# A tuned hybrid decoder layer on one core: the seventh and eighth input-projection weights of the first tile are loaded into a buffer of their own

## The chip, the core and the metric

The kernel runs on one core of a Trainium2 chip. The metric is device time in microseconds (us), from one execution of the whole program; the figure to beat is the median of three executions. The profile comes from one further execution.

Five engines work side by side, each through its own instruction list, strictly in the order of that list: TensorE (PE, with its weight loads PEld), VectorE (DVE), ScalarE (ACT), GpSimd (POOL) and SyncE (SP), which here does nothing but issue DMA transfers. An instruction that waits for a semaphore holds up all that stand behind it on its engine.

## The reference, cut to what matters

One decoder layer over 2048 tokens of 1024 channels, all in float32:

```python
hn   = rms_norm(x, mix_pre_g)
proj = hn @ w_in                              # q, k, v and the GLU input u
attn = sliding_window_attention(q, k, v, attn_sinks, rel_bias)
a, gate = split(u); c = a * sigmoid(gate)     # 512 channels
c = silu(layer_norm(causal_depthwise_conv31(c)))  @ w_conv_pw
h  = x + rms_norm(concat(attn, c) @ w_out, mix_post_g)
hn = rms_norm(h, ffn_pre_g)
h  = h + rms_norm((silu(hn @ w_gate) * (hn @ w_up)) @ w_down, ffn_post_g)
```

The change touches only the loading of a part of `w_in` for the first 512 tokens.

## The kernel before, in words

**Tiles.** The 2048 tokens are cut into four tiles of T = 512. Stage A of tile t (`stage_a`, names with `@A`) projects the tile with 14 units of `w_in`; a unit is 128 output channels, its weight a 128x1024 float32 block of 512 KB. Units 0 to 7 are the four GLU pairs (gate and value), 8 is k, 9 is v, 10 to 13 are q. Stage B (`@B`) is the attention of a tile, stage C (`@C`) its convolution, whose 31 taps run on DVE one by one into tiles called `fc`, stage W (`@W`) the output projection, stages H, F, G the feed-forward part. Stage J multiplies `w_conv_pw` with its half of `w_out` beforehand.

**Three products for one.** float32 accuracy is made from three passes of float32r: every operand is held as a high part and a low part. `split_w` (line 130) makes them from a raw weight: ACT copies the raw block to the high part (line 133), DVE subtracts that from the raw block to get the low part (line 136; it shows as line 85, the helper that records DVE operations), and SP stores the low part to HBM (`lo_in`, line 137), from where tiles 1 to 3 load it (line 132) instead of making it again. `three` (line 174) then issues, per 128 input channels, weight high by data high, weight high by data low, weight low by data high. So of each unit's 24 matmuls the first two need the high half alone and the third needs DVE's subtraction.

**The first tile.** Units 0 to 3 come as `w_four`, in quarters beside the first input blocks (`four`, line 343). From unit 4 on, `proj` (line 337) calls `kweight` (line 146), that calls `weight` (line 140), which takes a tile `raw` from a pool of two, has SP load the unit into it (line 143), and splits its two halves into two tiles `w` of a pool of six. As `raw` has two buffers, the load of unit 6 can't start before unit 4 has been split, nor that of unit 7 before unit 5 has been. The norm of the tile is applied after the first matmuls: `post` yields the row factors, and the GLU of the first pairs (`glu`, line 374; tiles `fa`) starts when they are there.

**What sets the order.** The order of each engine's list is not written by hand. The Tile framework schedules the recorded operations with priorities and a timeline of its own; lanes of side work (taps, attention, tails, joins) are pumped between the projections by estimated costs (`yield` values). A new or moved operation early on can so change the lists for a good while behind it. Taps have low priority and are put where DVE seems free.

**The tile `yt`.** It is a pool of one buffer, 128 x 2048 float32. Its users are stage J (line 702), the tails of the convolution (line 627) and the feed-forward part. In the trace stage J is the first that writes it, at 197.94 us.

Of the kernel before, what the change touches and what calls it, by code (L numbers as in the profile page):

```python
# [25 lines left out]
P = 128  # L26
T = 512
# [10 lines left out]
def layer_kernel(ctx, tc, x, xT, cols, rows, sinks, relb, onehot, w_in, w_four, w_pw, w_out, w_gate, w_up, w_down, out):  # L38
    nc = tc.nc
# [9 lines left out]
    def nm(s):  # L49
        uid[0] += 1  # L50
        return f"{s}@{lab[0]}_{uid[0]}"
# [3 lines left out]
    def t_(tag, shape, dt=F32):  # L55
        return sb.tile(list(shape), dt, tag=tag, name=nm(tag), bufs=BUFS[tag])
# [83 lines left out]
    def weight(src, low, made, raw=None, on_pool=True):  # L140
        if raw is None:
            raw = t_("raw", (P, 2, T))
            nc.sync.dma_start(raw, src)
        return [split_w(raw[:, n], "w", low[n], made, on_pool) for n in range(2)]

    def kweight(u, made, raw=None):
        hs = weight(w_in[u].rearrange("p (a b) -> p a b", a=2), lo_in[u], made, raw, False)
        return [(hs[k // 4][:, 0, (k % 4) * P : (k % 4 + 1) * P], hs[k // 4][:, 1, (k % 4) * P : (k % 4 + 1) * P]) for k in range(KC)]
# [41 lines left out]
    def three(o, pairs, first=True, last=True):  # L190
        n = 3 * len(pairs)
        i = 0
        for (sh, sl), (mh, ml) in pairs:
            for a, b in ((sh, mh), (sh, ml), (sl, mh)):
                mat(o, a, b, start=first and i == 0, stop=last and i == n - 1)
                i += 1
# [119 lines left out]
    def split_x(t, xs, rb, ks):  # L316
# [12 lines left out]
            hn.append(hk)  # L329
        return hn  # L330

    def stage_a(t, hn, done_with, hooks, post=None):
        L = f"A{t}"
        lab[0] = L
        rb = None

        def proj(u, bank_of=mm):
            w = kweight(u, t > 0)
            o = bank_of()
            for k in range(KC):  # L340
                three(o, [(w[k], (hn[k][:, 0], hn[k][:, 1]))], k == 0, k == KC - 1)
            return o
# [47 lines left out]
        for c in range(4):  # L390
            if post and c == 0:
                os = yield from four()
            if post and c < 2:
                continue
            og = proj(2 * c, tr if post and c == 2 else mm)
            if post and c == 2:
                rb = next(post)
                for j in range(2):
                    next(glu(j, *os[2 * j : 2 * j + 2]))
            half = glu(c, og, None)  # L400
            next(half)
            yield 5.2
            step(2 * c)
            half.send(proj(2 * c + 1, tr if post and c == 2 else mm))
            yield 5.2
            step(2 * c + 1)
        done_with("S")
        lab[0] = L
        ok = proj(8)
        if t:  # L410
            act(kz[:, :, 0:P], kz[:, :, T : T + P].bitcast(F32), AF.Copy)
# [1086 lines left out]
    for t in range(NT):  # L1498
        hooks = {}
        if t + 1 < NT:  # L1500
# [27 lines left out]
            if t < 2:  # L1528
                hooks.update({(9 if t == 0 else 8) + i: lambda i=i, f=pair_of: f(i) for i in range(4)})
        run(mark(stage_a(t, hn_a[t], (lambda n: lb.until(f"{n}{t-1}")) if t else (lambda n: None), hooks,  # L1530
                         None if t else norm_x(0, x0, sum_squares(0, x0))), f"A{t}"))
        for n, part in zip((f"S{t}", f"B{t}"), stage_b(t)):
# [97 lines left out]
```

## Time and profile before

| what | us |
|---|---|
| median of three executions | 1910.04 |
| lowest, highest | 1907.92, 1913.49 |
| the profiled execution, device time | 1913.71 |
| its span, first to last instruction | 1912.0 |
| outside of the span | 1.71 |
| PE busy in the span | 1889.1 (99%) |
| DVE busy | 1498.7 (78%) |
| ACT busy | 968.6 (51%) |
| POOL busy | 200.7 (10%) |
| mean share of the 16 DMA engines, 439.36 MB | 230 GB/s |
| mean granted PE clock | 0.999 of full speed |

In a row of the timeline stand the start and the length in us, the engine, the line, the operation, what it writes and reads by the program's names (number of the buffer left out), shapes and the count of merged instructions; in brackets how long the engine stood idle before it and who released it. A merged row's length reaches to the end of its last instruction, and PE's matmuls overlap: 128x512 matmuls follow each other at some 0.23 us although one takes 0.39 us. In the table of stages there stand the busy us and the counts of each engine, then the granted clock, the DMA share and the rate. In the list of waits stand the sum, the count and the longest.

### The profile page before, as it was taken

Reading aid. Unit: us, or ns where it says so; the run is one execution under the profiler, and the core shown is the slowest. Engines: PE = TensorE matmul, PEld = TensorE weight load, DVE = VectorE, ACT = ScalarE, POOL = GpSimd, SP = SyncE. Lnnn points to the kernel's source line nnn. Section 1 sums busy time; section 2 is a strip of 40 time slices with the busy share of each in tenths; the row PEclk is TensorE's granted clock in tenths of the full one; section 3 lists DMA queues with packets and bytes.
Section 4 is the critical chain, followed back from the end, with each engine's and each line's share of the span. In section 5 each row is a group of like instructions: output and inputs, shape, how many; then the busy total and the mean of one; then the engine's idle time right before and its main releaser. Section 6 shows DMA issues by size and latency. Waiting matters only on the chain.

```text
span 1912.0 us, 26682 instructions
## 1 busy us (share of the span) xinstructions
PE 1889.1 (99%) x8714; PEld 1530.7 (80%) x8714; DVE 1498.7 (78%) x2806; ACT 968.6 (51%) x1912; POOL 200.7 (10%) x247
## 2 busy tenths in 40 slices
PE   9999999999999999999999999999999999999998
PEld 7777777777778888887888888888888888888886
DVE  6999999998876999988999866787566665455558
ACT  5365445667567433433446583676443343345452
POOL 2010001210000000000000100010033233211002
PEclk9999999999999999999999999999999999999999
DMA  9886756769678776786696696798554543376663
GB/s 334 305 279 231 243 178 188 232 228 344 208 243 288 245 259 237 255 272 222 193 314 205 202 342 204 252 329 313 179 176 151 163 138 127 116 255 188 206 218 130
DMA packets 227644, 439.36 MB, mean 230 GB/s; under 512 B 22664, under 2 KB 48688, under 8 KB 227504
## 3 DMA queue, kind: packets, MB, share of 16 engines
q1 hardware_dynamic: 206192, 403.04, 63.5%
q10 hardware_dynamic: 19392, 28.32, 4.1%
q0 software_dynamic: 1920, 6.29, 0.9%
q8 instruction: 68, 1.11, 0.2%
q14 instruction: 72, 0.59, 0.1%
HBM read 318.54 MB, written 119.02 MB: 229 GB/s over the span
## 4 chain that ended last, share of the span: by engine, by line
PE 72%; DVE 14%; DMA 8%; issue 3%; ACT 1%; POOL 1%; SPq 1%; DVEq 0%; ACTq 0%; POOLq 0%
PE mm@F L108 38%; PE mm@G L108 19%; PE mm@A L108 6%; DVE fc@C L85 5%; PE tr@W L108 4%; PE mm@W L108 2%; PE tr@B L108 1%; DMA glu@C<-glu_scr 1%; DVE sm@G L85 1%; DMA chl@F<-w_gate 1%; DVE w@F L85 1%; DMA p@X<-w_four 1%; DVE tr@B L493 1%; DVE p@B L496 1%; DMA p@A<-x 1%
## 5 line engine op out<-in xcount | busy, mean ns | idle before, releaser
L85 DVE SCALAR_TENSOR_TENSOR fc@C<-glu@C,colt,fc@C 128x512 f32<-128x512 f32 x480 | 353.0, 752 | 1.6
L108 PE MATMUL mm@F<-hl@H,w@F 128*128 128x512 f32 x1056 | 254.4, 390 | 0.0
L108 PEld LDWEIGHTS mm@F<-hl@H,w@F 128*128 128x128 f32 x1056 | 197.9, 188 | 41.9 <-ACT fa@F L1049 0.8
L108 PE MATMUL mm@G<-hl@G,hl@G 128*128 128x512 f32 x924 | 227.6, 393 | 0.1
L891 ACT ACTIVATE w@F<-chl@F 128x512 fp32r<-128x512 f32 x220 | 135.6, 625 | 134.5 <-PE mm@F L108 128.9
L108 PE MATMUL mm@G<-w@G,hl@G 128*128 128x512 f32 x876 | 199.8, 389 | 0.6 <-DVE w@G L85 0.6
L108 PEld LDWEIGHTS mm@G<-hl@G,hl@G 128*128 128x128 f32 x924 | 171.3, 188 | 36.2 <-ACT hl@G L891 0.5
L108 PE MATMUL mm@A<-hl@A,w@A 128*128 128x512 f32 x792 | 193.3, 394 | 1.9 <-DVE w@A L85 1.7
L108 PEld LDWEIGHTS mm@G<-w@G,hl@G 128*128 128x128 f32 x876 | 164.3, 188 | 35.3 <-DVE w@G L85 1.0
L108 PEld LDWEIGHTS mm@A<-hl@A,w@A 128*128 128x128 f32 x792 | 146.6, 188 | 35.3 <-DVE w@A L85 2.2
L85 DVE TENSOR_TENSOR w@F<-chl@F,w@F 128x512 fp32r<-128x512 f32 x198 | 145.6, 739 | 32.7 <-ACT w@F L891 32.2
L108 PE MATMUL mm@F<-ql@H,w@F 128*128 128x512 f32 x528 | 130.4, 391 | 1.8 <-ACT w@F L891 1.4
L108 PE MATMUL mm@F<-mid@H,w@F 128*128 128x512 f32 x528 | 130.2, 390 | 0.0
L108 PE MATMUL mm@F<-p@H,w@F 128*128 128x512 f32 x528 | 129.2, 389 | 0.0
L108 PE MATMUL mm@F<-x@H,w@F 128*128 128x512 f32 x528 | 128.0, 391 | 0.0
L108 PEld LDWEIGHTS mm@F<-ql@H,w@F 128*128 128x128 f32 x528 | 98.4, 188 | 24.0 <-ACT w@F L891 2.3
L108 PEld LDWEIGHTS mm@F<-p@H,w@F 128*128 128x128 f32 x528 | 99.0, 188 | 20.8 <-ACT at@F L1149 0.4
L108 PEld LDWEIGHTS mm@F<-x@H,w@F 128*128 128x128 f32 x528 | 98.6, 188 | 21.1 <-issue 0.8
L108 PEld LDWEIGHTS mm@F<-mid@H,w@F 128*128 128x128 f32 x528 | 99.0, 188 | 20.5
L85 DVE TENSOR_TENSOR w@G<-raw@G,w@G 128x512 fp32r<-128x512 f32 x72 | 50.7, 705 | 67.5 <-ACT w@G L891 66.8
L108 PE MATMUL mm@W<-w@W,hl@W 128*128 128x512 f32 x384 | 97.9, 398 | 2.8 <-DVE hl@W L85 2.1
L133 ACT ACTIVATE w@A<-raw@A 128x512 fp32r<-128x512 f32 x104 | 63.0, 625 | 67.4 <-DMA raw@A<-w_in 38.4
(319 smaller groups left out, 3190.7 us busy)
## 6 DMA issues: line engine op xcount, KB each, us to landing
mids<-fa@F SPq DMA_DIRECT2D x154, 256.0 KB, 2.9
raw@A<-w_in SPq DMA_DIRECT2D x52, 512.0 KB, 5.6
w@A<-lo_in SPq DMA_DIRECT2D x84, 256.0 KB, 4.8
fa@G<-mids SPq DMA_DIRECT2D x74, 256.0 KB, 4.5
fc@G<-mids SPq DMA_DIRECT2D x72, 256.0 KB, 3.6
w@W<-lo_out SPq DMA_DIRECT2D x48, 256.0 KB, 5.0
chl@F<-w_gate SPq DMA_DIRECT2D x22, 512.0 KB, 4.0
raw@F<-w_gate SPq DMA_DIRECT2D x22, 512.0 KB, 4.3
```

The lines of the kernel that those rows point to most:

```text
L85: r = op(*args, **kw)
L108: r = nc.tensor.matmul(*args, **kw)
L133: act(w[:, 0], raw, AF.Copy)
L493: nc.vector.copy_predicated(os[g][:, :, P:], upper.unsqueeze(1).to_broadcast([P, 2, P]), prev)
L496: read = nc.vector.tensor_tensor_reduce(out=pr[:, h], in0=os[g][:, j, P:], in1=bias[0][:, h], op0=ALU.add, op1=ALU.max, scale=1.0, scalar=NEG,
L891: act(w[:, 0], x, AF.Copy)
```

## The change

For units 6 and 7 of the first tile the raw weights no longer go through the pool of two: they are loaded into the two halves of one tile `yt`, and `weight` is handed that tile. Splits, matmuls and stores stay the same in number and size. `raw` is so used by two units less, and the next units (8, 10, ...) take its buffers two turns sooner.

```diff
+    early_raw = []
+
     def stage_a(t, hn, done_with, hooks, post=None):
...
         def proj(u, bank_of=mm):
-            w = kweight(u, t > 0)
+            raw = None
+            if post and u in (6, 7):
+                if u == 6:
+                    early_raw.append(t_("yt", (P, 2, 2, T)))
+                raw = early_raw[0][:, u - 6]
+                nc.sync.dma_start(raw, w_in[u].rearrange("p (a b) -> p a b", a=2))
+            w = kweight(u, t > 0, raw)
```

What the scheduler makes of it is seen in the lists. Lines behind the change read 8 higher there; a name is the tile's tag, its stage and running numbers. All five lists differ from before over their first third: on PE up to instruction 2642 of 8635, behind which the lists agree to the end; DVE's differ up to 1158 of 2808, SP's up to 366 of 1293.

**SP, from the load of unit 5 on.** Before, `raw@A_70` is unit 5, `raw@A_75` unit 6; `p@A` and `x@A` are inputs of the second tile, `wx@J` a weight of stage J:

```order
L143 DMA raw@A_70_465<-w_in 128x1024
L262 DMA x@A_35_286<-xT 128x2x512
L276 DMA p@A_65_441<-x 128x1024
L262 DMA x@A_36_288<-xT 128x2x512
L276 DMA p@A_66_444<-x 128x1024
L687 DMA wx@J_340_2173<-w_out 128x1024
L137 DMA lo_in<-w@A_48_359 128x512
L137 DMA lo_in<-w@A_49_363 128x512
L143 DMA raw@A_75_509<-w_in 128x1024
```

and now, where `yt@A_75` are units 6 and 7 and `raw@A_88` is unit 8:

```order
L143 DMA raw@A_70_465<-w_in 128x1024
L262 DMA x@A_35_286<-xT 128x2x512
L345 DMA yt@A_75_509<-w_in 128x1024 x2
L276 DMA p@A_65_441<-x 128x1024
L262 DMA x@A_36_288<-xT 128x2x512
L276 DMA p@A_66_444<-x 128x1024
L695 DMA wx@J_339_2172<-w_out 128x1024
L137 DMA lo_in<-w@A_48_359 128x512
L137 DMA lo_in<-w@A_49_363 128x512
L143 DMA raw@A_88_608<-w_in 128x1024
```

Units 6 and 7 moved up by six and nine issues, and three inputs of the second tile, stage J's weight and the stores of unit 4's low half stand two issues later.

**DVE, after the row factors of the first tile.** Before, with `w@A_76`, `w@A_77` the low halves of unit 6, `w@A_84` of unit 7, `fa@A` the GLU's and `sm@A` the second tile's norm:

```order
L85 TENSOR_TENSOR fa@A_53_399<-mm@A_23_177,gb@A_52_397 128x512
L85 SCALAR_TENSOR_TENSOR fa@A_54_402<-fa@A_53_399,mm@A_24_178 128x512
L85 TENSOR_TENSOR fa@A_55_406<-mm@A_25_179,gb@A_52_397 128x512
L85 SCALAR_TENSOR_TENSOR fa@A_56_409<-fa@A_55_406,mm@A_26_180 128x512
L85 TENSOR_TENSOR fa@A_57_413<-tr@A_50_367,gb@A_52_397 128x512
L85 TENSOR_TENSOR w@A_76_511<-raw@A_75_509,w@A_76_511 128x512
L85 TENSOR_SCALAR gb@A_88_604<-ident,sm@A_68_448 128x128 x4
L85 TENSOR_TENSOR w@A_77_515<-raw@A_75_509,w@A_77_515 128x512
L85 TENSOR_TENSOR w@A_84_562<-raw@A_83_560,w@A_84_562 128x512
```

and now, where `w@A_83` and `w@A_84` are unit 7:

```order
L85 TENSOR_TENSOR fa@A_53_399<-mm@A_23_177,gb@A_52_397 128x512
L85 TENSOR_TENSOR w@A_76_511<-yt@A_75_509,w@A_76_511 128x512
L85 SCALAR_TENSOR_TENSOR fa@A_54_402<-fa@A_53_399,mm@A_24_178 128x512
L85 TENSOR_TENSOR fa@A_55_406<-mm@A_25_179,gb@A_52_397 128x512
L85 TENSOR_SCALAR sm@A_67_447<-sm@A_62_434 128x4
L85 TENSOR_SCALAR sm@A_68_448<-sm@A_67_447 128x4
L85 TENSOR_TENSOR w@A_77_515<-yt@A_75_509,w@A_77_515 128x512
L85 TENSOR_SCALAR sm@A_68_448<-sm@A_68_448 128x4
L85 SCALAR_TENSOR_TENSOR fa@A_56_409<-fa@A_55_406,mm@A_26_180 128x512
L85 TENSOR_TENSOR fa@A_57_413<-tr@A_50_367,gb@A_52_397 128x512
L85 TENSOR_TENSOR w@A_83_561<-yt@A_75_509,w@A_83_561 128x512
```

The low half of unit 6 stood behind five GLU operations and stands behind one. On ACT the four copies of units 6 and 7 stood two behind the second and two behind the third of the first tile's GLU activations (line 377); now one stands ahead of the first, one between the first and the second, and two between the second and the third.

**PE, at the end of the output projection of the second tile (stage W1).** Before, `tr@B_855` is the last matmul of an attention score, `mm@W_934` to `mm@W_940` are the first products with the last two input blocks `hl@W_898`, `hl@W_899`, and `ct@H` transposes for the feed-forward part:

```order
L108 MATMUL tr@B_855_5117<-kz,ql@A_788_4763 128x256
L538 MATMUL tr@B_878_5229<-ident,p@B_810_4866 128x128 x4
L909 MATMUL ct@H_907_5348<-ident,fa@H_906_5346 128x128 x4
L108 MATMUL mm@W_934_5478<-w@W_932_5472,hl@W_898_5319 128x512 x2
L108 MATMUL mm@W_935_5487<-w@W_932_5472,hl@W_898_5319 128x512 x2
L108 MATMUL mm@W_936_5496<-w@W_932_5472,hl@W_898_5319 128x512 x2
L108 MATMUL mm@W_940_5516<-w@W_932_5472,hl@W_898_5319 128x512 x2
L538 MATMUL tr@B_885_5260<-ident,p@B_810_4866 128x128 x4
L909 MATMUL ct@H_916_5392<-ident,fa@H_915_5390 128x128 x4
L108 MATMUL mm@W_934_5478<-w@W_932_5472,hl@W_898_5319 128x512
```

and now, where `tr@B_855` is the first matmul of that score and `hl@W_897` the block:

```order
L917 MATMUL ct@H_886_5269<-ident,fa@H_885_5267 128x128
L108 MATMUL mm@W_925_5443<-w@W_900_5326,hl@W_848_5094 128x512 x3
L108 MATMUL mm@W_925_5443<-w@W_901_5329,hl@W_849_5097 128x512 x3
L917 MATMUL ct@H_894_5307<-ident,fa@H_893_5305 128x128 x4
L917 MATMUL ct@H_906_5347<-ident,fa@H_905_5345 128x128 x4
L108 MATMUL mm@W_933_5477<-w@W_931_5471,hl@W_897_5318 128x512 x2
L108 MATMUL mm@W_934_5486<-w@W_931_5471,hl@W_897_5318 128x512 x2
L108 MATMUL mm@W_935_5495<-w@W_931_5471,hl@W_897_5318 128x512 x2
L108 MATMUL mm@W_939_5515<-w@W_931_5471,hl@W_897_5318 128x512 x2
L108 MATMUL tr@B_855_5117<-kz,ql@A_771_4645 128x256
```

The eight products that need only the high part of the block moved from behind the twelve score matmuls to ahead of them.

Further places, by their number in the lists: the last tap of the second tile's convolution is instruction 744 of DVE's list before and 787 now, and PE's transposes of that result (line 605) begin their last four at 1857 before and 1908 now. Stage W0's first matmul is 1514 on PE before and 1498 now; the first addition of its results on DVE (tile `x@W`) 727 before and 708 now. ACT's list has two loads of its function table more than before (three of them, where one stood, around the last softmax of tile 3).

## The prediction

> **What bounds the kernel now.** I read the page's first part and its chain first.
>
> ```profile
> span 1912.0 us, 26682 instructions
> PE 1889.1 (99%) x8714; PEld 1530.7 (80%) x8714; DVE 1498.7 (78%) x2806; ACT 968.6 (51%) x1912; POOL 200.7 (10%) x247
> PE 72%; DVE 14%; DMA 8%; issue 3%; ACT 1%; POOL 1%; SPq 1%; DVEq 0%; ACTq 0%; POOLq 0%
> ```
>
> PE is busy for 1889.1 of 1912.0 us. The change takes no matmul away, so it can win only from the 22.9 us in which PE stands idle, and it loses wherever a changed list makes PE wait anew. The list of PE's waits in the first 700 us, the stretch that holds every changed instruction, says what there is:
>
> ```profile
> PE tr@B L108 <- DVE sm@B L496: 2.8, 3, 1.1
> PE mm@W L108 <- DVE hl@W L85: 2.1, 1, 2.1
> PE mm@A L108 <- DVE w@A L85: 1.7, 1, 1.7
> ...
> PE mm@A L108 <- DVE x@W L85: 0.9, 1, 0.9
> PE mm@W L108 <- DVE x@W L85: 0.7, 1, 0.7
> PE tr@B L108 <- POOL p@B L541: 0.7, 1, 0.7
> ```
>
> The third row is the wait that the change is about. The first, second and the last three, 2.8 + 2.1 + 0.9 + 0.7 + 0.7 = 7.2 us, lie in stages whose order is shuffled by the way. The table of stages shows what else is scarce:
>
> ```profile
> 20.00:30.00 10.00, 10.00 (x49) 8.09 (x48) 4.44 (x11) 2.09 (x3) 1.50 (x2) 1.00 1.03 406
> 30.00:40.00 10.00, 10.00 (x48) 8.26 (x47) 5.71 (x21) 6.76 (x12) 1.57 (x8) 1.00 1.03 400
> 40.00:50.00 10.00, 8.26 (x36) 6.29 (x35) 7.14 (x13) 3.34 (x6) 5.12 (x9) 1.00 0.81 245
> 60.00:350.00 290.00, 288.59 (x1456) 223.97 (x1455) 277.19 (x626) 150.99 (x373) 25.53 (x44) 1.00 0.70 233
> 350.00:400.00 50.00, 47.39 (x249) 36.14 (x248) 48.41 (x116) 26.97 (x70) 6.92 (x12) 1.00 0.69 228
> ```
>
> The DMA engines are full from 20 to 40 us (share 1.03). PE's only hole there is in 40 to 50 us. From 60 to 400 us DVE (third pair) is busy 277.19 of 290 and 48.41 of 50 us: where PE waits there, it waits for work that DVE was given late. The granted clock is 1.00 throughout.
>
> **The change part by part.** First the wait itself, from the timeline around it:
>
> ```profile
> 35.91 5.74 PE L108 MATMUL tr@A<-hl@A,w@A 128*128 128x512 f32 x24
> 35.96 1.06 ACT L277 ACTIVATE junk<-p@A 128x1024 bf16<-128x1024 f32 x1 [0.67 <-DMA p@A<-x]
> ...
> 36.45 0.42 SPq L143 DMA_DIRECT2D raw@A<-w_in  x1
> ...
> 37.02 0.58 ACT L313 ACTIVATE gb@A<-ct@A 128x512 f32<-128x512 f32 x1
> ...
> 37.63 0.69 DVE L85 TENSOR_TENSOR fa@A<-mm@A,gb@A 128x512 f32<-128x512 f32 x1
> ...
> 40.88 1.14 ACT L133 ACTIVATE w@A<-raw@A 128x512 fp32r<-128x512 f32 x2
> ...
> 41.55 0.73 PE L108 MATMUL mm@A<-hl@A,w@A 128*128 128x512 f32 x2
> 41.62 0.68 DVE L85 TENSOR_TENSOR fa@A<-tr@A,gb@A 128x512 f32<-128x512 f32 x1
> ...
> 42.16 1.26 POOL L385 TENSOR_TENSOR fa@A<-fa@A,gb@A 128x512 f32<-128x512 f32 x1
> 42.22 1.76 DVE L85 TENSOR_TENSOR w@A<-raw@A,w@A 128x512 fp32r<-128x512 f32 x1
> ...
> 44.03 2.33 PE L108 MATMUL mm@A<-hl@A,w@A 128*128 128x512 f32 x9 [1.74 <-DVE w@A L85]
> ```
>
> Unit 5's 24 matmuls run from 35.91 to 41.55, (41.55 - 35.91) / 24 = 0.235 us each. Unit 6 starts on time; its third matmul needs the low half and is due at 41.55 + 2 x 0.235 = 42.02. It starts at 44.03, so **the wait costs 2.0 us** of PE's flow (the 1.74 leaves out the pipelined tail of the second matmul). The raw block isn't what is late at the end: ACT copies it at 40.88 without a wait, because its list puts the copy behind two GLU activations, and DVE's list puts the subtraction behind five GLU operations.
>
> When would the blocks be there now? These are SP's issues of that stretch and the landing times of line 276, all of the same size, 512 KB:
>
> ```profile
> 23.25 0.33 SPq L276 DMA_DIRECT2D p@A<-x  x1
> 23.75 0.38 SPq L262 DMA_DIRECT2D x@A<-xT  x1
> 24.22 0.49 SPq L276 DMA_DIRECT2D p@A<-x  x1
> ...
> DMA to landing us min/median/max: 9.3/10.0/11.7
> ```
>
> The two loads take the places of the issues at 23.25 and 23.75 and so land about 33 to 35 us, in place of one load issued at 36.45 and one ahead of it. ACT is through with the row factors at 37.6, takes the first copy (half of 1.14) and is done by 38.2; DVE is done with its one GLU operation at 38.3, and the low half is there by about 39.0, 3 us ahead of 42.02. The second half of the block is due 12 matmuls into the unit, at 41.55 + 12 x 0.235 = 44.4; ahead of it ACT now has an activation and the square of the last `p@A`. That row landed at 35.96 and is pushed by two blocks of 0.52 MB: 1.05 MB at 403 GB/s (the mean of 406 and 400) take 2.6 us, so it lands at 38.6. With 1.06 for the square and 0.6 for the copy it is split by 41.5. Unit 7 has 5.6 us more. So the wait goes whole, **-2.0 us**; nothing else of PE's is late next, as units 8 and 10 get their `raw` buffers two turns sooner.
>
> The Trainium skill speaks against moving loads into that stretch: "DMA: Bandwidth & Descriptors", section Specifications, gives about 358 GB/s as a core's limit to HBM. The two rows at 400 and 406 GB/s say that it is not reached as a wall here; by its figure the push would be 2.9 us instead of 2.6, an estimate from that page, and the sum would be the same.
>
> What is pushed behind: three inputs of the second tile, needed for a norm that PE applies some 20 us later, and stage J's weight, needed much later still. Nothing, with that cover; without it up to the 2.6 us.
>
> Second, **the shuffled lists** between 45 and about 590 us. Copies, subtractions, matmuls and stores are the same in number. Two table loads more on ACT are bounded by the one that the trace has:
>
> ```profile
> 538.45 1.28 ACT L1049 ACT_TABLE_LOAD   x1
> ```
>
> that is 0 to 2.6 us; ACT is half idle (968.6 of 1912), so I take 0. The place that I can follow through the rows is the end of stage W1:
>
> ```profile
> 504.73 0.67 ACT L929 ACTIVATE chl@H<-ct@H,colt 128x512 f32<-128x512 f32 x1
> ...
> 505.70 0.98 PE L108 MATMUL tr@B<-kz,ql@A 64*128 64x256 f32 x12 [1.10 <-DVE sm@B L496]
> 505.81 0.63 ACT L932 ACTIVATE hl@H<-chl@H 128x512 fp32r<-128x512 f32 x1 [0.40 <-ACT chl@H L929]
> ...
> 506.34 1.13 ACT L785 ACTIVATE hl@W<-mb@J 128x512 fp32r<-128x512 f32 x2
> ...
> 511.79 1.28 DVE L85 TENSOR_TENSOR hl@W<-mb@J,hl@W 128x512 fp32r<-128x512 f32 x2
> ...
> 512.52 0.74 PE L108 MATMUL mm@W<-w@W,hl@W 128*128 128x512 f32 x2 [2.10 <-DVE hl@W L85]
> ```
>
> Two waits, 1.10 + 2.10 = 3.2 us. Now eight W1 products stand ahead of the score, so PE comes to the score some 8 x 0.235 = 1.9 us later and that 1.10 goes; DVE's subtraction of the block stands sooner behind the score's reads, so the 2.10 mostly goes too. But the eight products need ACT's copy at 506.34, and ACT's list reaches that through two rounds of activation, copy and a feed-forward weight's copy, about 2 x (0.67 + 0.63 + 0.63) + 0.6 = 4.5 us behind the last transposes (a weight's copy taken as the 0.63 of line 932's, of the same size), while PE has six products and eight transposes of a quarter of their width, (6 + 2) x 0.235 = 1.9 us. That is a new wait of 2.6 us against 3.2 gone. Ends: -3.2 (ACT ahead by then) and +1.3 (another round of 1.9); I take **0**, as the two nearly meet. The other waits of the list, 7.2 - 3.2 = 4.0 us, can vanish or double, -4.0 to +4.0; I take **0** for them, since DVE stays as full as its rows show.
>
> Sum: -2.0 us against the profiled execution of 1913.7 us (span 1912.0 and 1.7 outside). That execution lies 3.7 us over the median of the three timed, 1910.0, so against the median: **1908.0 us**.
>
> **The rivals.**
>
> *More goes than the one wait (faster).* DVE's first addition in W0 stands 19 instructions sooner, PE's first W0 matmul 16 sooner: by the rows of 350 to 400 us that is 19 x 48.41 / 116 = 7.9 us against 16 x 47.39 / 249 = 3.0, DVE gains 4.9 us on PE just where PE waited for `x@W`. Against it: what was moved ahead there was taken out of the taps, which come back later. The price: -2.0 and all of the 7.2, -9.2 at best; half of the 7.2 gives -5.6 and **1904**, most of it 1902.
>
> *The convolution of the second tile comes late (slower).* Its last tap stands 43 instructions later on DVE, 43 x 48.41 / 116 = 17.9 us, its reader on PE 51 later, 51 x 47.39 / 249 = 9.7 us.
>
> ```profile
> 365.10 0.74 DVE L85 SCALAR_TENSOR_TENSOR fc@C<-glu@C,colt,fc@C 128x512 f32<-128x512 f32 x1
> 365.87 0.32 SPq L621 DMA_DIRECT2D y_scr<-fc@C  x1
> ...
> 379.31 0.41 SPq L633 DMA_DIRECT2D fc@C<-y_scr  x1
> ...
> 391.55 0.59 PEld L605 LDWEIGHTS ct@C<-ident,fc@C 128*128 128x128 f32 x4
> ```
>
> Before there were 391.55 - 365.87 = 25.7 us between store and reader; now 25.7 - (17.9 - 9.7) = 17.5. The way through HBM took 13.4 us to the second issue, mostly SP's queue. SP holds its list at the store until DVE has made the tap, with weights of tile 4 behind it, and PE's list holds at the transposes. From 17.5 - 13.4 = 4 us more delay of the taps on, each us costs PE one; as much again as the 8.2 lost and 4 more, 12 - 4 = 8 us, gives **1916**.
>
> *The blocks land no earlier, or the subtraction is slow all the same (the change doesn't do what it says).* The split at 42.22 took 1.76 us where the one at 37.63, as large, took 0.69, beside POOL's multiplication of 1.26 us: 1.07 of the 2.0 us are that neighbour. So even with the block late, another place in the list gains about 1 us, and a collision in the new place costs 1 of the 3 us to spare. 1909 to **1910**. The Trainium skill, "SBUF — State Buffer", section "SBUF: two separate sides", says of this that a VectorE operation with two SBUF inputs and a GpSimd operation that reads SBUF exclude each other from a shared port for a whole instruction; the two rows agree (1.76 is 0.69 and most of 1.26).
>
> **How the numbers follow.** The forecast with its 2.0 us: 0.46. More waits gone: 0.21. The late convolution, or another wait of that sort in the shuffled third: 0.25. Nothing gained: 0.08. A measurement of this kernel can tell about 0.3%, 5.7 us, from no change: faster means under 1904.3, slower over 1915.8. The second case lies mostly under 1904.3 (0.16 of 0.21) and the forecast's lower tail adds 0.04; the third lies over 1915.8 for 0.20 of 0.25, and the upper tail of the others adds 0.03. So faster 0.20, same 0.57, slower 0.23. The range: to 1901 below (the 7.2 us gone but for 2), to 1917 above (the late convolution with 1 us more). The forecast's own range is 1904 to 1912, its 2.0 and the 4.0 of the unknown waits.
>
> **What would show it.** Right: after the 24 `tr@A` matmuls unit 6 and 7 run through, 48 at 0.235, without a bracket; the first `w@A<-yt@A` on DVE ends near 39 us; PE's busy time between 40 and 50 us is 10.0. Wrong: a bracket `<-DVE w@A` or `<-ACT w@A` on PE there. For the shuffled part: the rows of `hl@W` and `sm@B` in PE's waits, and whether a row `ct@C ... L605` has a bracket. The prediction fails if PE's waits between 60 and 600 us, 7.2 us by the list and some tenths unlisted, come out over 11 or under 3.5.

## The result, and the profile after

| | median, us | lowest to highest | executions |
|---|---|---|---|
| before | 1909.01 | 1903.53 to 1913.49 | 12 |
| after | 1913.68 | 1912.28 to 1916.32 | 12 |

The ratio is 1.0025 [1.0017, 1.0034]: the change makes the kernel **4.7 us slower**, less than the 0.3% that the prediction called "same", but on the other side of zero from the forecast of -2.0. The median of before is now that of 12 executions, the three of the earlier table among them.

The page of the changed kernel hides this:

```profile
span 1912.4 us, 26677 instructions
PE 1889.5 (99%) x8714; PEld 1533.4 (80%) x8714; DVE 1499.5 (78%) x2806; ACT 971.9 (51%) x1914; POOL 200.1 (10%) x247
PE 94%; DVE 3%; DMA 2%; ACT 1%; issue 1%; ACTq 0%; DVEq 0%; POOL 0%; SPq 0%; POOLq 0%
```

The spans differ by 0.4 us (1912.4 against 1912.0). The profiled execution of before, at 1913.71, lies just above before's twelve, that of after, at 1914.07, in the middle of its own. So two pages can't be subtracted here; the traces must be compared at the same instruction. The lists agree again behind PE's instruction 2642; this row stands behind that point, first in before, then in after:

```profile
554.61 1.03 PE L538 MATMUL tr@B<-ident,p@B 128*128 128x128 f32 x8
```

```profile
559.18 1.03 PE L546 MATMUL tr@B<-ident,p@B 128*128 128x128 f32 x8
```

After is 4.57 us behind there, as much as the medians differ. That the two agree so closely is partly luck: a second profile of before (e9 below) passes this row at 551.56. What made the spans alike came later, in the part of the program that the change doesn't touch: behind this row before's execution took 4.2 us more than after's, of which the lists of waits explain 2.2 (3.7 against 1.5 us behind 600 us).

Where was it lost? The stages of after (us, then busy us and counts of PE, PEld, DVE, ACT, POOL, then the granted clock, the DMA share, GB/s):

```profile
40.00:50.00 10.00, 10.00 (x46) 8.29 (x45) 7.96 (x16) 5.79 (x11) 6.27 (x16) 1.00 0.82 290
...
60.00:350.00 290.00, 290.00 (x1465) 225.65 (x1462) 277.86 (x624) 153.20 (x374) 27.09 (x45) 1.00 0.71 234
350.00:400.00 50.00, 42.57 (x216) 32.63 (x214) 44.34 (x99) 22.90 (x62) 6.98 (x11) 1.00 0.66 206
...
450.00:500.00 50.00, 47.84 (x246) 38.21 (x245) 39.80 (x109) 34.28 (x82) 1.10 (x2) 0.97 0.96 331
500.00:550.00 50.00, 47.90 (x249) 35.14 (x248) 48.89 (x123) 33.92 (x73) 3.63 (x5) 0.97 0.56 187
```

and those of before that weren't shown:

```profile
450.00:500.00 50.00, 50.00 (x269) 39.32 (x268) 40.05 (x110) 32.17 (x77) 1.75 (x2) 1.00 0.95 328
500.00:550.00 50.00, 46.80 (x241) 35.37 (x240) 47.43 (x122) 35.53 (x85) 3.08 (x4) 1.00 0.53 177
```

Until 350 us the change does better than was forecast: PE is full from 40 to 50 us (8.26 before) and from 60 to 350 (288.59). Counted one by one in the traces (the tables count a matmul that lies across two rows twice), PE has then started 1724 matmuls against 1705, 19 more, or 19 x 0.227 = 4.3 us of lead. From 350 to 550 it starts 954 against 993, 39 fewer, 8.9 us lost. Net 4.5 us behind: the two halves of the story. The list of PE's waits in the first 700 us names the second (the same sum, count and longest as before):

```profile
PE ct@C L613 <- ACT yt@C L614: 3.2, 1, 3.2
PE mm@W L108 <- ACT fa@A L387: 2.9, 1, 2.9
PE mm@W L108 <- ACT mid@W L768: 2.2, 1, 2.2
PE ct@X L108 <- POOL ident masks.py:199: 1.6, 1, 1.6
PE ct@H L917 <- ACT chl@H L937: 1.2, 1, 1.2
PE mm@W L108 <- ACT hl@W L793: 0.9, 1, 0.9
PE ct@C L613 <- DMA fc@C<-y_scr: 0.7, 1, 0.7
PE mm@A L108 <- DVE x@W L85: 0.7, 1, 0.7
```

Every large wait of before is gone (`sm@B` 2.8, `hl@W` from DVE 2.1, `w@A` 1.7). Without the fourth row, which belongs to the start of the kernel, 11.8 us stand between 60 and 600 us where 7.2 stood, and 10.4 of them name ACT. ACT is busy for half of the span; it is late by the order of its list and by what that order waits for.

**Around 360 us (2.9).** The rows that lead to the first of these waits, in order of time:

```profile
352.52 0.69 DVE L85 SCALAR_TENSOR_TENSOR fc@C<-fc@C,fc@C 128x512 f32<-128x512 f32 x1
353.24 0.32 SPq L674 DMA_DIRECT2D mixT<-fc@C  x1
357.41 0.32 SPq L815 DMA_DIRECT2D fa@W<-mixT  x1
361.68 0.63 ACT L793 ACTIVATE hl@W<-fa@W 128x512 fp32r<-128x512 f32 x1 [5.35 <-DMA fa@W<-mixT]
362.21 0.58 ACT L387 ACTIVATE fa@A<-mm@A 128x512 f32<-128x512 f32 x1
362.85 3.96 PE L108 MATMUL mm@W<-w@W,hl@W 128*128 128x512 f32 x16 [2.85 <-ACT fa@A L387]
```

The last product of a convolution block of the **first** tile (DVE, 352.52) goes to HBM and comes back as an input of W0, 361.68 - 352.52 = 9.2 us later. ACT stands in its list at that block's copy for 5.35 us, and an activation behind it has to free a PSUM bank that PE needs (a bank holds a product of PE until another engine has read it). Who is named (`fa@A`) is the one behind the one that is late. Before, ACT waited for the same input later, and PE waited for no row of ACT there:

```profile
363.56 0.59 ACT L379 ACTIVATE fa@A<-mm@A 128x512 f32<-128x512 f32 x1
...
367.90 0.63 ACT L785 ACTIVATE hl@W<-fa@W 128x512 fp32r<-128x512 f32 x1 [3.23 <-DMA fa@W<-mixT]
```

So the input comes 6.2 us sooner in after, but W0 stands sooner too, and now the activation that frees the bank stands behind the late copy, not ahead of it.

**Around 384 us (0.7 and 3.2).** The second tile's convolution, the place of the second rival:

```profile
369.97 0.32 SPq L674 DMA_DIRECT2D mixT<-fc@C  x1
370.38 3.60 SPq L641 DMA_DIRECT2D fc@C<-y_scr  x2
374.53 0.42 SPq L143 DMA_DIRECT2D raw@A<-w_in  x1
375.13 0.66 PE L613 MATMUL ct@C<-ident,fc@C 128*128 128x128 f32 x4 [0.73 <-DMA fc@C<-y_scr]
382.83 0.63 ACT L133 ACTIVATE w@A<-raw@A 128x512 fp32r<-128x512 f32 x1 [8.68 <-DMA raw@A<-w_in]
383.36 0.58 ACT L614 ACTIVATE yt@C<-ct@C 128x512 f32<-128x512 f32 x1
383.99 0.65 PE L613 MATMUL ct@C<-ident,fc@C 128*128 128x128 f32 x4 [3.20 <-ACT yt@C L614]
```

The transposes of block 1 ran at 375.13 into the only bank `ct`. ACT's copy out of it needed 0.58 us and could have run at 375.8, but it stands behind the copy of a weight whose load SP issued at 374.53, behind a store of the first tile, and ACT waited 8.68 us for that. The transposes of block 2 had to wait for the bank.

**Around 469 us (2.2), and the clock behind it.** The same pattern in W1: ACT copies a weight that has just come from HBM, and the copy that frees a bank for PE stands behind it:

```profile
467.82 0.63 ACT L133 ACTIVATE w@W<-raw@W 128x512 fp32r<-128x512 f32 x1 [1.92 <-DMA w@W<-lo_out]
468.87 0.58 ACT L768 ACTIVATE mid@W<-mm@W 128x512 f32<-128x512 f32 x1
469.50 7.39 PE L108 MATMUL mm@W<-w@W,hl@W 128*128 128x512 f32 x24 [2.16 <-ACT mid@W L768]
```

24 matmuls take 7.39 us there, not 5.7. The granted clock says why:

```profile
469.50:471.00 1.50, 1.50 (x6) 1.24 (x7) 1.00 (x2) 1.45 (x3) 0.00 (x0) 1.00 1.04 416
471.00:474.40 3.40, 3.40 (x9) 2.64 (x8) 3.29 (x9) 2.23 (x4) 0.00 (x0) 0.50 1.03 414
474.40:478.00 3.60, 3.60 (x24) 2.73 (x23) 2.07 (x4) 1.20 (x2) 0.00 (x0) 1.00 0.98 335
512.00:515.40 3.40, 3.18 (x8) 2.48 (x8) 3.40 (x10) 1.89 (x4) 0.00 (x0) 0.51 0.40 131
```

For 3.4 us after the wait PE has half its clock, and again at 512, behind the waits at the end of W1. Each stretch costs half of its length, 1.7 us, which no list of waits shows: PE is "busy" in it. So from 350 to 550 us: PE's idle time by the tables is 11.7 us now and 5.8 before, 5.9 more, and two half-clock stretches make 3.4: 9.3, near the 8.9 counted in matmuls.

Over all executions the mean granted clock is 0.9972 after and 0.9984 before (12 executions, and the 23 that ran beside e1 to e4). Times the length that is 5.4 and 3.1 us: of 5.3 us between the means of these executions, 2.3 are clock and 3.0 the rest.

### The profile page after: what moved, and what is told of

It reads as the page before. It is cut to its first block, busy times and chain, and to the rows that moved or that the text cites. A ratio compares the mean times of both kernels' runs of the same rounds, so it can differ in the third digit from the quotient of the medians.

```text
span 1912.4 us, 26677 instructions
## 1 busy us (share of the span) xinstructions
PE 1889.5 (99%) x8714; PEld 1533.4 (80%) x8714; DVE 1499.5 (78%) x2806; ACT 971.9 (51%) x1914; POOL 200.1 (10%) x247
## 4 chain that ended last, share of the span: by engine, by line
PE 94%; DVE 3%; DMA 2%; ACT 1%; issue 1%; ACTq 0%; DVEq 0%; POOL 0%; SPq 0%; POOLq 0%
PE mm@F L108 44%; PE mm@G L108 19%; PE mm@A L108 15%; PE tr@W L108 4%; PE mm@W L108 4%; PE tr@B L108 3%; PE ct@J L108 1%; DVE sm@G L85 1%; PE tr@B L546 1%; PE tr@A L108 1%; PE tr@H L917 1%; DMA raw@A<-w_in 0%; DMA raw@W<-w_out 0%; DVE x@G L85 0%; PE ct@C L613 0%
```

## The experiments

**Theory.** The new place of the blocks does gain its 2 us and more; the loss is made by the *order* that the scheduler found for the rest, on ACT and SP above all. **Rival 1**: the loads pushed in at 23 us cost what they displace. **Rival 2**: the lead is worth nothing in any order, as DVE and ACT are full behind it.

To test an order, the list of each engine was tied to a sequence written down in the kernel, by dependencies that only order and wait for nothing. Both kernels emit the same instructions, so that either can be given the other's lists, cut and joined at one matmul, or single rows moved. The edit to the kernel is the same each time, and what varies is the sequence:

```diff
-        layer_kernel(tc, *aps, out)
+        layer_kernel(tc, *aps, out); pin(tc, unpack(ORDER))
...
+def pin(tc, order):
+    ins = list(tc.nc.cur_bb.bb.instructions)
+    for row in order:
+        for a, b in zip(row, row[1:]):
+            tc.add_manual_dep(ins[b], ins[a].name,
+                mybir.DependencyInfo(mybir.DependencyClass.NoSync, mybir.DependencyReason.DATA),
+                reason="pinned order")
```

Below "old" and "new lists" are those of before and of after. Each ratio is to executions of before made beside the run.

### Both halves of the change apart

**e1**: new loads and new lists for PE's first 290 matmuls (some 70 us in the trace, not 64), old lists behind.

> The kernel after, but every engine's list behind the first 290 matmuls of PE (about 64 us) goes in the order of the kernel before: the moved loads, and the splits of units 6 and 7 in their new places, without the reshuffle of 64 to 590 us. Theory L (the lists): the loads gain the 2.0 us of the wait at 42 us, and the loss comes from the new order behind. So 2.0 us under before, ratio 0.999, PE's only larger waits behind 64 us those of before (score of B at 505, hl@W at 512), no stretch at half clock. Theory D (the pushed transfers and the earlier turns of raw): the loss goes with the loads, so 3 to 5 us over before, ratio 1.002 to 1.003.

Measured 1907.96, **0.9996 [0.9987, 1.0005]**: neither the 2.0 us under before nor the 3 to 5 over it. The loss isn't there, and the gain can't be told. **e2**: the mirror, old loads and lists for the first 290 matmuls, new lists behind.

> The kernel before with its loads through the pool of two and its lists up to the 290th matmul, and the lists of after from there. Theory L: it has the wait at 42 us (2.0 us) and the loss of the new lists too, so 4.7 + 2.0 = 6.7 us over before, ratio 1.0035, with the waits for yt@C (3 us), fa@A (3 us) and mid@W (2 us) of after, and a mean clock of 0.997. Theory D: as before, within 1 us.

Measured 1916.25, **1.0041 [1.0027, 1.0054]**. So the whole loss sits in the rearranged rest, and rival 1 is out as its cause: with the old loads it is larger. The start is worth 1.0041 - 1.0025 = 0.16%, 3 us, under the new lists (their intervals overlap), but nothing that can be told under the old ones. Against before's trace e1 leads by 2.4 us at the 290th matmul (66.01 against 68.39 us) and by 0.3 at 110:

```profile
110.66 3.06 PE L108 MATMUL mm@A<-mid@A,w@A 128*128 128x512 f32 x12 [1.37 <-ACT w@A L133]
```

ACT's list has that weight's copy behind the eight exponentials of a score that came no sooner; PE arrived early, and waited.

**e3**: new lists up to the 1500th matmul (some 320 us in the trace, not 335), old lists behind, to see whether the loss begins before or after that.

> The kernel after with its lists up to the 1500th matmul (about 335 us), and the order of before from there. Theory L in its narrow form (the loss is made by the order of the stages W0, C1 and W1 themselves, 350 to 520 us): 2.0 us under before, as the run with the cut at 64 us. In its wide form (the taps and copies that the lists of 64 to 335 us put off are missing later, in whatever order): 2 to 5 us over before. Theory D: 3 to 5 us over before.

Measured 1916.48, **1.0039 [1.0026, 1.0052]**, 7.8 us slower, more than any of the three numbers, and for a reason of its own:

```profile
PE tr@B L108 <- DVE sm@B L504: 8.5, 2, 8.0
```

At the seam the taps that the new lists had put off stand all at once on DVE, ahead of a score's reductions. It doesn't place after's loss, but it shows that the smooth stretch from 60 to 350 us is partly bought on credit: work of DVE is put off to a later place, as the prediction's second rival said.

**e4**: only the two loads moved on SP, everything else in the old order.

> The kernel after with all lists of before but SP's, in which only the two loads of units 6 and 7 stand at their new place. ACT's copy of unit 6 stands behind two GLU activations and DVE's subtraction behind five GLU operations, as before. If the place in the lists set the wait, a bracket of 1 to 2 us stays on PE at 42 us and the time is 0 to 1 us under before. If the landing of the block set it, the bracket goes and the time is 2.0 us under. Theory D: 3 to 5 us over before.

Measured 1912.79, **1.0026 [1.0017, 1.0034]**, 4.1 us slower: what rival 1 had named, 3 to 5 us. So with the old lists the loads do cost what they displace. The target wait doesn't go but grows, by the lists of waits from 1.7 us to 4.7:

```profile
44.08 0.73 PE L108 MATMUL mm@A<-hl@A,w@A 128*128 128x512 f32 x2 [2.97 <-ACT w@A L133]
46.56 3.68 PE L108 MATMUL mm@A<-hl@A,w@A 128*128 128x512 f32 x9 [1.75 <-DVE w@A L85]
```

and ACT's rows say why:

```profile
38.50 1.06 ACT L277 ACTIVATE junk<-p@A 128x1024 bf16<-128x1024 f32 x1 [0.94 <-DMA p@A<-x]
...
43.41 1.14 ACT L133 ACTIVATE w@A<-yt@A 128x512 fp32r<-128x512 f32 x2
```

The pushed `p@A` lands at 38.50 instead of 35.96, a push of 2.54 us (the prediction had 2.6), and holds ACT's old list, with the GLU activations and both copies behind it. The push is real; in after the scheduler's new list, which takes the first copy ahead of that row, hides it. A half-clock stretch follows at 46.1 us (and another comes at 377.2). The 3.0 us more of waiting and the clock come to 4.1 by the medians.

### Mending the rest

In e5 to e7 the changed kernel has its own lists with single rows moved. **e5**: on ACT the copy out of `ct` ahead of the weight's.

```diff
+L614 ACTIVATE yt@C_589_3633<-ct@C_591_3636 128x4x128
 L133 ACTIVATE w@A_689_4140<-raw@A_688_4138 128x512
-L614 ACTIVATE yt@C_589_3633<-ct@C_591_3636 128x4x128
+L614 ACTIVATE yt@C_589_3633<-ct@C_593_3644 128x4x128
 L133 ACTIVATE w@A_690_4143<-raw@A_688_4138 128x512
-L614 ACTIVATE yt@C_589_3633<-ct@C_593_3644 128x4x128
```

> The kernel after with all its lists, but on ACT the copies of the second tile's convolution result (line 614, first and second block) stand one place sooner, each ahead of the copy of a projection weight of the fourth tile, for which ACT waited 8.7 us. Theory L1 (the place in ACT's list makes the wait): PE's 3.2 us for yt@C go and stay gone, 3 us under after (1910.7), with less time at half clock if the next window had one. Theory L2 (PE only meets the next late work sooner): the 3.2 us come back in the waits at 467 and 510 us, and the time is within 1 us of after (1913 to 1914).

Measured 1912.53, **1.0023 [1.0014, 1.0032]**, which can't be told from after's 1.0025. The 3.2 went, and at the same transposes stood the block's own way through HBM:

```profile
PE ct@C L613 <- DMA fc@C<-y_scr: 2.6, 1, 2.6
```

**e6**: on ACT the copy that frees the bank in W1 ahead of two weights' copies.

```diff
+L768 ACTIVATE mid@W_788_4775<-mm@W_797_4797 128x512
 L133 ACTIVATE w@W_836_5023<-raw@W_835_5021 128x512
 L133 ACTIVATE w@W_837_5026<-raw@W_835_5021 128x512
-L768 ACTIVATE mid@W_788_4775<-mm@W_797_4797 128x512
```

> The kernel after, but on ACT the copy that empties a bank of W1's products (line 768, mid@W) stands ahead of the two copies of a weight that is still on its way, at 467 us. L1: the wait of 2.2 us falls to some 0.7, and as PE then idles less than half of a clock window, the stretch of 3.4 us at half clock behind it goes too: 1.5 + 1.7 = 3 us under after. L2: within 1 us of after. If the half clock costs nothing by itself: 1.5 us under.

Measured 1911.72, **1.0018 [1.0009, 1.0027]**. The wait fell from 2.2 to 0.8 and the half-clock stretch behind it was gone (its execution had two others, at 363 and 383 us). That is 2.0 us under after, between the two expectations, and the intervals overlap.

**e7**: both of these, and on DVE and SP the product of the first tile's block and its store sooner (the 2.9), and on ACT a transposed block's copy ahead of a weight's (the 1.2).

```diff
+L85 SCALAR_TENSOR_TENSOR fc@C_498_3127<-fc@C_497_3125,fc@C_498_3127 128x512
 L85 TENSOR_TENSOR p@B_530_3316<-p@B_530_3316,sm@B_538_3372 128x512 x2
...
-L85 SCALAR_TENSOR_TENSOR fc@C_498_3127<-fc@C_497_3125,fc@C_498_3127 128x512
...
+L674 DMA mixT<-fc@C_498_3127 128x512
 L815 DMA fa@W_622_3804<-mixT 128x512
 L143 DMA raw@W_675_4072<-w_join 128x2x512
-L674 DMA mixT<-fc@C_498_3127 128x512
...
-L899 ACTIVATE w@F_954_5592<-raw@F_951_5583 128x512
 L937 ACTIVATE chl@H_895_5312<-ct@H_894_5307,colt 128x512
 L938 DMA hT_4770<-chl@H_895_5312 128x512
+L899 ACTIVATE w@F_954_5592<-raw@F_951_5583 128x512
```

> The kernel after with both moves, and two more: at 352 us DVE's product of the first tile's second convolution block ahead of two multiplications, and its store on SP ahead of a load (PE waits 2.9 us for that block at 360 us); at 509 us ACT's copy chl@H ahead of a weight's copy (PE waits 1.2 us). L1: 3.2 + 3 + 2.9 + 0.5 = 9.6 us under after, 1904, which is 5 us under before. L2: what is gained at 360 and 384 us is lost again at the next rendezvous with DVE, 1908 to 1911.

Measured 1909.54, **1.0002 [0.9993, 1.0011]** against after's 1.0025. The waits on `fa@A` and `mid@W` are gone; in their place:

```profile
PE ct@C L613 <- DMA fc@C<-y_scr: 2.9, 2, 2.0
...
PE mm@W L108 <- ACT hl@W L793: 1.4, 1, 1.4
```

Six rows moved, with loads and splits as in after, take the loss away: 4.1 us, less than half of the 9.6 that the four waits add up to. By its list PE waits 7.3 us between 60 and 600 us, after 11.8, before 7.2. That the loss hangs on the order of these six rows together is shown; what each of them is worth isn't. **e10** went on from e7, with SP's loads of the second tile's convolution ahead of a store and a weight, and the feed-forward weight's copy on ACT behind the two copies `hl@W`:

```diff
-L674 DMA mixT<-fc@C_513_3208 128x512
 L641 DMA fc@C_590_3634<-y_scr 128x512
 L641 DMA fc@C_592_3642<-y_scr 128x512
+L674 DMA mixT<-fc@C_513_3208 128x512
...
+L641 DMA fc@C_594_3650<-y_scr 128x512
 L143 DMA raw@W_706_4259<-w_join 128x2x512
-L641 DMA fc@C_594_3650<-y_scr 128x512
...
-L899 ACTIVATE w@F_954_5592<-raw@F_951_5583 128x512
...
 L793 ACTIVATE hl@W_898_5321<-mb@J_340_2174 128x512
+L899 ACTIVATE w@F_954_5592<-raw@F_951_5583 128x512
```

> The mended after with three more moves: on SP the first two loads of the second tile's convolution result ahead of the store of the first tile's last block, the third ahead of a 512 KB weight, and on ACT a feed-forward weight's copy behind hl@W. PE's waits there in the mended run were 0.9 + 2.0 us for these loads and 1.4 us for hl@W. L1 (each wait has its place in a list): 3 us and a stretch of half clock in some runs under the mended run, 1905 to 1906.5, 3 us under before. L2 (the loads are late because the DMA engines are busy, and what is gained is lost again at the next rendezvous): within 1 us of it, 1908.5 to 1910.

Measured 1910.89, **1.0004 [0.9995, 1.0014]**. A miss: the blocks came no sooner (`ct@C` from DMA 4.1 us in two waits, 2.9 in e7). SP's place was not what held them.

### What the start is worth

**e9** is the control: before, with its own order written down.

> The kernel before, with the order of every list written down as it was and nothing else changed: a second profile of the same program, and a test of the way in which the other runs fix their order. Ratio 1.000 within 0.1%. If the profile of before was an unlucky execution behind 555 us (it lost 4.2 us there against after's), this one has fewer of the waits of PE for w@F and gb@F between 650 and 900 us, and the same waits as before up to 555 us. If the stage behind 600 us always gives back what the front gains, it has them too.

Measured 1908.29, **0.9993 [0.9983, 1.0003]**: writing an order down costs nothing that can be told. Its profiled execution has a span of 1904.2 us, that of before 1912.0, with the same instructions in the same order; in it the wait on `hl@W` is 0.7 us (2.1) and that on `sm@B` 1.1 (2.8); all waits from 60 to 600 us add up to 3.7 us (7.2). The prediction had put such waits down as the kernel's own.

**e8**: e1, with the late copy at 107 us ahead of the exponentials on ACT, and DVE's two subtractions `hl@W` at 506 us sooner.

```diff
+L133 ACTIVATE w@A_193_1240<-raw@A_192_1238 128x512
+L133 ACTIVATE w@A_194_1243<-raw@A_192_1238 128x512
 L524 ACTIVATE p@B_141_962,sm@B_148_1008<-p@B_141_962,sm@B_146_1003 128x128 x8
...
-L133 ACTIVATE w@A_193_1240<-raw@A_192_1238 128x512
-L133 ACTIVATE w@A_194_1243<-raw@A_192_1238 128x512
```

> The run with the new lists for the first 64 us and the old ones behind, with two moves: at 107 us ACT's two copies of a weight ahead of eight softmax operations (PE, being 1.8 us ahead there, waited 1.4 us for them and lost its lead), and at 506 us DVE's two subtractions of hl@W ahead of those of a feed-forward weight (PE waited 1.9 us). L1: 1.4 + 1.9 us, and 1.7 us of half clock in the runs that had it, under that run: 1904. L2 (DVE is what sets the pace from 60 to 400 us): the lead is lost at another place behind 110 us, and only the 1.9 us remain: 1906.

Measured 1909.31, **1.0003 [0.9994, 1.0012]**. The lead was lost earlier still, on DVE:

```profile
75.42 3.12 DVE L85 SCALAR_TENSOR_TENSOR fc@C<-glu@C,colt,fc@C 128x512 f32<-128x512 f32 x4
78.45 1.29 DVE L85 TENSOR_TENSOR w@A<-raw@A,w@A 128x512 fp32r<-128x512 f32 x2
```

Four taps stand ahead of the subtraction that PE waits for (1.68 us at 79.19).

**e12, e13, e14** test whether DVE's load is what eats the lead: before's lists, e1's and after's, with 24 of the 31 taps of the first tile cut to 8 columns. The convolution of the first tile is so left incomplete in all three, and they are compared with each other.

```diff
-                stt(y, g[:, j : j + T], dwh[:, c, j : j + 1], y, ALU.mult, ALU.add)
+                n = T if t or j > 6 else 8
+                stt(y[:, 0:n], g[:, j : j + n], dwh[:, c, j : j + 1], y[:, 0:n], ALU.mult, ALU.add)
```

> The kernel before with its order written down, and 24 of the first tile's 120 later taps (the first six of each channel block) cut from 512 columns to 8, so that the first tile's convolution is incomplete: DVE has 24 x 0.6 = 14 us less to do between 60 and 200 us, in the same order. Base for the two runs beside it. Theory P (DVE sets the pace from 60 to 400 us): PE's waits of 60 to 340 us go too, and the time falls by 1 to 4 us. Theory N (it doesn't): as before within 1 us.

> The new lists for the first 64 us and the old ones behind, with the same 24 taps cut to 8 columns (the first tile's convolution is incomplete). In the whole kernel this start gained 2.2 us at 42 us and had lost most of it by 140 us, 0.7 us remained. Theory P: with DVE relieved the lead is not met by a late subtraction at 78 or 110 us, and stays: 2.0 to 2.5 us under the old order with the same taps cut. Theory N: 0.7 us under it, with the lead lost by 140 us all the same.

> The kernel after with its order written down and the same 24 taps cut to 8 columns (the first tile's convolution is incomplete). Theory P: what the lists of after put off on DVE between 60 and 335 us is there in time now; the wait of 2.9 us at 360 us shrinks as DVE gives the convolution block sooner, and the loss of 4.7 us against the old order with the same taps falls below 2. Theory N: the loss stays at 4 to 5 us, as the waits at 360 to 510 us hang on ACT's and SP's order alone.

Measured 1908.25 (**0.9996 [0.9987, 1.0005]**), 1906.39 (**0.9985 [0.9975, 0.9994]**) and 1913.65 (**1.0028 [1.0016, 1.0039]**). Relieving DVE alone gains nothing that can be told (e12). With DVE relieved the new start keeps 1.9 us between the medians, as much as the removed wait (the means of 11 executions each are 3.1 +- 2.0 us apart; those of e1 and before 0.1 +- 1.6), and after's rearranged rest loses as much as ever, 5.4 us over e12; its wait on `yt@C` is 2.9 us (3.2), that on `fa@A` 2.2 (2.9). So the gain seems to hang on room on DVE, as far as these margins can show it; the loss doesn't. Both rival 2 (in part) and the theory stand, each for its half.

**e15**: e8 with all taps, and on DVE the subtractions at 75 us ahead of two taps.

```diff
-L85 SCALAR_TENSOR_TENSOR fc@C_61_426<-glu@C_60_423,colt,fc@C_61_426 128x512 x4
+L85 SCALAR_TENSOR_TENSOR fc@C_61_426<-glu@C_60_423,colt,fc@C_61_426 128x512 x2
 L85 TENSOR_TENSOR w@A_122_826<-raw@A_121_824,w@A_122_826 128x512
+L85 SCALAR_TENSOR_TENSOR fc@C_61_426<-glu@C_60_423,colt,fc@C_61_426 128x512
 L85 TENSOR_TENSOR w@A_123_830<-raw@A_121_824,w@A_123_830 128x512
```

> The whole computation with the new lists for 64 us and the old ones behind, and three small moves: at 75 us DVE's two subtractions of a projection weight ahead of three and two taps (PE, 2 us ahead, met them late by 0.5 and 1.7 us in two executions), at 107 us ACT's two copies of a weight ahead of eight softmax operations, at 506 us DVE's subtractions of hl@W ahead of those of a feed-forward weight. Theory P, as the runs with fewer taps bore it out (a lead of PE lasts only where DVE's list gives it the next operand in time): the lead of 2.2 us holds to 335 us and beyond, 2 to 3 us under before, ratio 0.9985 to 0.999. Theory N (the lead is met somewhere else): within 1 us of before.

Measured 1907.84, **0.9993 [0.9983, 1.0003]**: not told apart from before, and equal to e9. No order of the whole computation that was tried here can be told from before on the fast side. The starts of the same matmuls show how far the lead lives, in us:

```
             290th   score at 79   score at 336  score at 372   554
before       68.39      79.13        336.67       372.77     554.61
e9           69.47      80.21        335.85       371.62     551.56
e1           66.01      76.75        335.68       371.24     554.02
e15          65.75      76.49        334.87       370.62     549.62
e12 (light)  68.31      79.06        334.69       371.00     552.29
e13 (light)  67.02      77.77        333.60       368.56     548.86
```

e15's trace holds 1.9 us over e9's at the last point, its time doesn't show it. Before and e9, one program, lie 3.0 us apart there, so a single trace decides nothing of that size.

**e11**: only unit 6 through `yt`, and the scheduler free to order as it likes.

```diff
-            w = kweight(u, t > 0)
+            raw = None
+            if post and u == 6:
...
+            w = kweight(u, t > 0, raw)
```

> The kernel after, but only unit 6 is loaded into the buffer of its own, unit 7 goes through the pool of two, and the scheduler is free to order the lists. Theory L (the loss is what the scheduler happens to make of the lists): the wait at 42 us goes, and the rest of the time bears no relation to how much was moved; the waits between 300 and 560 us stand at other places than in after, and the time lies anywhere from 1903 to 1917. Theory D (the loss grows with the bytes that are pushed): half of after's loss, 1911 to 1912.

Measured 1911.49, **1.0009 [0.9999, 1.002]**. Half of the edit rearranged even more of the program (in the traces PE's order is that of before again from the 4043rd matmul on, in after from the 2719th), and the waits came out in other places (`mm@F` from ACT 2.1, `sm@B` 2.0, `mid@W` 1.8). The median lies where rival 1 had put it (1911 to 1912), the theory had allowed anything from 1903 to 1917, and the interval holds 1: this run decides between them in no way. It shows that the order changes with any such edit.

## Why the prediction was right or wrong

**The wait that goes (-2.0): right at its place.** The 48 matmuls run through, and the row of 40 to 50 us has PE at 10.0. The first copy comes ahead of the square of the pushed `p@A`, which runs at 39.74 us, the second right behind it:

```profile
38.23 0.62 ACT L133 ACTIVATE w@A<-yt@A 128x512 fp32r<-128x512 f32 x1
39.09 0.68 DVE L85 TENSOR_TENSOR w@A<-yt@A,w@A 128x512 fp32r<-128x512 f32 x1
```

The low half is there at 39.77, "by about 39.0" in the forecast. By the start of unit 7 PE is 2.2 us ahead.

**"Nothing else of PE's is late next": wrong** for the old order behind it. The step looked at units 7, 8 and 10. e1 and e8 find what is late next at 79 us (DVE's subtraction behind taps) and at 110 (ACT's copy behind exponentials); e13, where DVE has room, keeps 1.9 us between the medians. The view for it was on the table: with DVE busy for 277.19 of 290 us, a lead of PE is also a lead on DVE.

**The pushed transfers (nothing): right in after.** The price without a cover, "up to 2.6 us", was too low, and the cover isn't only that the norm is needed later, as the prediction had it: in e4 the push of 2.54 us holds ACT's list, adds 3.0 to the very wait that was to go, and 4.1 to the time.

**Table loads of ACT (0): right.** They stand between 538 and 556 us, and PE isn't kept waiting there.

**The end of W1 (-3.2 and +2.6, taken as 0): the mechanism right,** the new waits 1.2 + 0.9 = 2.1, both behind ACT's rounds (0.9 on `hl@W`, as said, 1.2 on `ct@H`). The half-clock stretch of 1.7 us at 512 was not in it.

**"The other waits" (4.0, taken as 0 with ends of -4.0 and +4.0): this is the step that failed.** They came to 9.7 us (11.8 less W1's 2.1), 5.7 more, beyond the worse end. The reason given was that DVE stays as full. DVE did; the new waits don't come from it. They come from ACT's list, with a bank's copy behind a weight that is still on its way (3.2, 2.2), and from a block that DVE, SP and HBM hand on (2.9, 0.7): 9.0 us between 360 and 470 us, where before's table of stages has 2.6 us of idle time from 350 to 500. "ACT is half idle" was used for the table loads and was true, but an engine in strict order can be half idle and late. The criterion that the prediction had named for its failure, waits over 11 us, is met (11.8). e7 shows the cause by undoing it, for the six rows together.

**Rival 2 (the convolution late)** came true at its row `ct@C`, but by another road and at half its price. It looked at the last tap, which comes 28 us later (393.76 against 365.87 for its store); the fourth block's transposes, at 404.27, stand only 10.5 us behind that store and didn't wait, so the 13.4 us taken for the way through HBM were too many. Blocks 1 and 2 did wait, 0.7 + 3.2 us: the 3.2 is ACT's order by name, but in e5, with that order put right, the same transposes wait 2.6 us for the block itself. How much of the blocks' own delay is SP's queue and how much the transfers' stays open, as e10 gained nothing by SP's order. **Rival 1 (more waits gone)** had W0 right as far as DVE goes: `x@W` is down from 0.7 and 0.9 to one wait of 0.7. It left out that W0's own inputs come through HBM. **"Doesn't do what it says"** didn't happen. **The range** has a slip: its lower end of 1901 is the sum with all of the 7.2 us gone (1910.0 - 9.2), not all but 2.

**The clock: left out altogether.** The prediction took "1.00 throughout" as given. A price for half clock belonged to every new wait of 2 us or more; it is 2.3 of the 5.3 us between the means.

## What to carry to other kernels

Where a scheduler orders the lists, price a change by the lists that it makes, not by the edit: for each place where PE's rows move, go through ACT's and SP's rows for a copy that frees a bank and stands behind something that comes from HBM. A lead of PE is kept only as far as the engines that feed it have room, so look at the next 50 us of the fullest of them before a removed wait is counted. And where executions of one program spread over 10 us, compare two traces at the same instruction behind the change, and trust the medians for the rest.

## What the runs showed of the hardware

**Half clock comes in whole windows, after waits well short of one.** In 17 traces of this study each half-clock stretch, but for the last one at the end of the execution, is 3.413 us long, or two or three times that, and they begin on a grid of 3.413 us that runs through the execution whatever the program does. Matmuls follow each other at 0.427 us in them instead of 0.227, so that one costs 1.7 us. Sorted by how long PE wasn't busy in a window at full clock (the last 20 us of an execution left out):

```
idle in the window, us    windows    next window at half clock
1.9 and more                 12               12
1.46 to 1.9                  14                4
under 1.46             all others              0
```

A wait of 2 to 3 us so costs 1.7 us more or nothing, by where it falls: the 3.2 at 384 us lay across two windows and cost nothing more in after, while waits at that place in e5, e6 and e7 did. The Trainium skill, "TensorE: Matmul & The Clock Gate", section "Part 1: The HAM clock gate", gives the same free-running window of 3413 ns, and half clock after at least one idle window of about 3.4 us. These traces agree on the window and differ on the rest, as 1.9 us of idle time in one, 56% of it, was enough each time.

**One order, two traces, 7.8 us apart.** Before and e9 run the same instructions in the same order, with spans of 1912.0 and 1904.2 us. They part by 3.0 us up to the matmul at 554 us and by 4.7 behind it, where before has 3.7 us of listed waits (behind 600 us) and e9 1.2. What sets this in an execution wasn't settled.
